# The first modulation's products turned round: weights stationary, the two conditioning vectors moving, and the stream loads dealt out between the weight loads

## The chip, the cores and the metric

One core of a Trainium2 chip runs the whole network in one launch. The metric is the device time of that launch in microseconds (us). TensorE (PE) multiplies a stationary 128x128 block, loaded into it by a weight load (PEld), by moving columns. VectorE (DVE), ScalarE (ACT) and GpSimd (POOL) do the elementwise work, and SyncE (SP) issues most transfers.

## What is computed

Four layers work on 512 latent tokens and 256 context tokens of width 1024. Ahead of each half layer both streams are normalised and modulated by shifts and scales that come from a conditioning vector: `c` for the latent tokens, `c_ctx` for the context. Cut to what matters here (layer 0, first half):

```python
sh1, sc1, ... = split(silu(c) @ ada_w + ada_b, 6)
ch1, cc1, ... = split(silu(c_ctx) @ ada_w + ada_b, 6)
xn  = rmsnorm(h, g1) * (1 + sc1) + sh1
xcn = rmsnorm(hc, g1) * (1 + cc1) + ch1
y, yc = short_conv_mixer(xn, ...), short_conv_mixer(xcn, ...)   # begins with x @ w_in
```

Nothing can be multiplied by `w_in` until the streams, their norms and the shift and scale of a channel block are there.

## The kernel before

Activations are kept channel-major, eight tiles of 128 channels per stream: `hL0` to `hL7` (128x512, the latent stream) and `hC` (128x256 each, the context). Most products are made from two rounded halves of each operand (`xh`, `xl`, `wh`, `wl`), three matmuls per product (`mm3`).

The opening of the program, up to about 60 us, is what the change touches. `run` calls `setup` and then steps a generator, `ada_first`. For each of the eight channel blocks j it loads the 256 weight columns of that block (128 for the shift, 128 for the scale) as two tiles `adaf{j}_0` and `adaf{j}_1` of 512 KB, from a pool of five buffers (tag `raw`). Before, `cwide` holds silu of the two vectors, each copied 64 times, so that it fills a 128x128 stationary block, and the 256 weight columns move past it in full float32: eight matmuls per j (the profile shows each float32 matmul as two records, each with a weight load of its own). The result has the two vectors along the partitions, so ScalarE copies it to `adarow` and TensorE turns it by two transposes. VectorE then adds the bias (`md`) and makes the gain (`gs`).

```python
raw = self.first.tile([P, KC // 2, 2 * P], F32, name=f"adaf{j}_{i}", tag="raw", bufs=5)
...
nc.tensor.matmul(acc[:, :2 * P], self.cwide[:, i * KC // 2 + k], raw[:, k], ...)
```

After `lead` blocks (2 before) `load_h` issues the loads of both streams: 8 pieces of context, 8 of x. Then three norms are begun, of the context and of the latent tokens' two halves (`norm_steps` with `first` set): ScalarE squares each channel tile (`nsq`), VectorE adds the squares (`nacc`), TensorE sums over channels with a column of ones (`nps<-ones,nacc`, 2 moving columns), POOL takes the power (`rstd`), TensorE spreads it over partitions (`nps<-identr,rstd`), and VectorE multiplies (`nt`). For each j, as soon as `md` and `gs` are there, ScalarE makes `xh`, POOL scales `nt`, and VectorE makes `xl`, three times (context, two halves).

The products of the first mixer for the context and the first latent half are issued ahead (`phase_start`, tiles `pre0` and `pre1`); they are the first consumers of `xh` and `xl`.

A scheduler orders the instructions of each engine; transfers on SP keep the program's order where the code asks for it. Each engine runs its own list in order.

Of the kernel before, what the change touches and what calls it, by code (L numbers as in the profile page):

```python
# [9 lines left out]
F32 = mybir.dt.float32  # L10
# [4 lines left out]
PSUM = bass.MemoryType.PSUM  # L15

P = 128
PRM = dict(res1=6, pg0=140, pg1=180, dir=2, wx=0, pin=0, plo=((), ()), nb=2, nl=4, lead=2, nadd='DDD', mid=(0, 0, 0), rope='PP', c1w=7, l1w=8, o1=16, s1=0, r1=6, pf0=17, pf1=33, vd1=7, ord=0, w2=12, o2=24, s2=7, v2=6, r2=8, res=2, kp=0, vp=18, t0=5, t1=4, t2=3, t3=3, ks='A', ksl='D', st='A', stl='P', qT2='A', oraw='A', qs='A', qsl='D', qT1='A', mh='A', ml='P', m='A', kT='A', vh='A', vl='P', comb='P')
KEEP = (2, 3, 4)
EARLY = (4, 5)  # L20
PADS = (32, 56)
XPAD = 48
D = 1024
KC = D // P
# [23 lines left out]
class Trunk:  # L48
# [101 lines left out]
    def cpy(self, k, out, x):  # L150
        e = PRM[k]
        if e == "A":
# [4 lines left out]
    def tt(self, k, out, a, b, op):  # L157
        (self.nc.vector if PRM[k] == "D" else self.nc.gpsimd).tensor_tensor(out, a, b, op)

# [73 lines left out]
        hC = [self.hC2[k // 2][:, k % 2, :] for k in range(KC)]  # L233
        self.h = {0: hL, 1: hC}

    def load_h(self):
        for k in range(KC):
            self.tc.keep_in_program_order(self.nc.sync.dma_start(self.h[1][k], self.A["ctx"][k]))
        for k in range(KC):
            self.tc.keep_in_program_order(self.nc.sync.dma_start(self.h[0][k], self.A["x"][k]))  # L240


    def ada_vecs(self, l, m):
# [2 lines left out]
    def ada_first(self):  # L246

        nc = self.nc
        for j in range(KC):
            if j in EARLY:  # L250
                self._fetch(True)
                self._split()
            acc = self.pb(f"adaf{j}")
            for i in range(2):
                raw = self.first.tile([P, KC // 2, 2 * P], F32, name=f"adaf{j}_{i}", tag="raw", bufs=5)
                self.tc.keep_in_program_order(nc.sync.dma_start(raw, self.A["l0_ada_first"][j, i]))
                for k in range(KC // 2):
                    nc.tensor.matmul(acc[:, :2 * P], self.cwide[:, i * KC // 2 + k], raw[:, k],
                                     start=i + k == 0, stop=i * k == KC // 2 - 1)
            row = self.ntmp("adarow")[:, :2 * P]  # L260
            nc.scalar.copy(row, acc[:, :2 * P])
            for m in range(2):
                nc.tensor.transpose(acc[:, (2 + m) * P:(3 + m) * P], row[:, m * P:(m + 1) * P], self.ident)
            cols = acc[:, 2 * P:].rearrange("p (m v e) -> p m v e", m=2, v=2)[:, :, :, 0]
            md = self.first.tile([P, 2, 2], F32, name=f"md{j}", tag="md", bufs=KC)
            nc.vector.tensor_tensor(md, cols, self.ada_b[0][:, 0:2, j:j + 1].to_broadcast([P, 2, 2]), ALU.add)
            gs = self.first.tile([P, 2], F32, name=f"gs{j}", tag="gs", bufs=KC)
            nc.vector.scalar_tensor_tensor(gs, md[:, 1, :], 1.0, self.g1[0][:, j:j + 1].to_broadcast([P, 2]),
                                           ALU.add, ALU.mult)
            self.mods1.append((md[:, 0, :], gs))  # L270
            yield
# [45 lines left out]
    def norm_steps(self, l, s, second, first):  # L317
# [16 lines left out]
        acc = self.ntmp("nacc")[:, :T]  # L334
        direct = 0 if first else PRM["dir"]
        sums = [acc]
        for k in range(KC):
# [6 lines left out]
            else:  # L344
                sq = self.ntmp("nsq")[:, :T]
                nc.scalar.activation(sq, h[k], AF.Square)
                (nc.vector if first and PRM["nadd"][2 * off // SEQ if sid == 0 else 2] == "D" else nc.gpsimd).tensor_tensor(acc, acc, sq, ALU.add)
            yield
# [27 lines left out]
        for k, (hi, lo) in enumerate(xs):  # L376
# [5 lines left out]
            else:  # L382
# [3 lines left out]
                nc.scalar.activation(hi, t1, AF.Identity, bias=sh)  # L386
            if not first and k in PRM["plo"][sid]:
                nc.scalar.activation(t1, t1, AF.Identity, bias=sh)
# [26 lines left out]
    def phase_start(self, srcs, xn, regions):  # L415

        n = PRM["nb"] if len(regions) == 2 else PRM["nl"]
        self.pre = [self.project(src, xn, parts_of(regions)[:-1], f"pre{i}", split=i >= 2) for i, src in enumerate(srcs[:n])]
# [716 lines left out]
    def run(self):  # L1135
        tc, nc = self.tc, self.nc
        es = ExitStack()
        self.setup(es)
        dp = es.enter_context(tc.tile_pool(name="arow", bufs=1, space=bass.MemoryType.DRAM))
        self.arow = dp.tile([12 * DEPTH, D], F32, name="adarows")  # L1140
        self.plan_weights()
        adac = tc.tile_pool(name="ada", bufs=1, side=self.yside)
        self.adap = adac.__enter__()
        cw = self.adap.tile([P, KC, 2, P // 2], F32, name="cwide", tag="ar", bufs=2)
        nc.vector.tensor_copy(cw, self.cpair[:, :, :, None].to_broadcast([P, KC, 2, P // 2]))
        self.cwide = cw.rearrange("p k v e -> p k (v e)")
        stc = tc.tile_pool(name="first", bufs=1, side=self.yside)
        self.first = stc.__enter__()
        self.mods1 = []
        ada = self.ada_first()  # L1150
        for _ in range(PRM['lead']):
            next(ada)
        self.load_h()
        self.xc = None
        self.xside = "left"
        self.xn_next = None
        self.next = (0, REGIONS, False)
        norms = [self.begin(s, True) for s in parts_of(REGIONS)]
        for i, nrm in enumerate(norms):
            for _ in range(PRM['mid'][i]):  # L1160
                next(ada)
            while next(nrm) != "stats":
                pass
        for j in range(KC):
            if len(self.mods1) <= j:
                next(ada)
            for nrm in norms:
                next(nrm)
        for _ in ada:
            pass  # L1170
        stc.__exit__(None, None, None)
        self.ada = self.ada_run([(0, m) for m in (2, 4, 3)])

        phases = [(0, REGIONS, False), (0, REGIONS, True), (1, REGIONS, False), (1, REGIONS, True),
                  (2, REGIONS, False), (2, (LAT,), True), (3, (LAT,), False), (3, (LAT,), True)]
        for i, (l, streams, second) in enumerate(phases):
            xn, self.xn_next = self.xn_next, None
            self.next = phases[i + 1] if i + 1 < len(phases) else None
            if l % 3 == 0 and not second:
                yc = tc.tile_pool(name=f"y{i}", bufs=1, side=self.yside)  # L1180
                y = yc.__enter__()
                self.pads(y, streams)
                self.conv_mixer(l, xn, streams, y, ticks=PRM['t0'])
            elif not second:
                (self.window_gqa if l == 1 else self.diff_attn)(xn)
            else:
                if l % 3:
                    yc = tc.tile_pool(name=f"y{i}", bufs=1, side=self.yside)
                    y = yc.__enter__()
                    self.pads(y, streams)  # L1190
                if l == 0:
                    self.ada = self.ada_run([(0, 5)] + [(1, m) for m in (1, 0, 2, 4, 3, 5)])
                if l in (1, 2):
                    adac = tc.tile_pool(name=f"ada{l}", bufs=1, side=self.yside)
                    self.adap = adac.__enter__()
                    self.ada = self.ada_run([(l + 1, m) for m in (1, 0, 2, 4, 3, 5)])
                self.ffn(l, xn, streams, y, ticks=PRM[f't{l + 1}'] if l < 3 else 3)
                self.tick(1000)
                if l == 0:
                    self.ada = self.ada_run([(0, 5)] + [(1, m) for m in (1, 0, 2, 4, 3, 5)])  # L1200
                if l in (1, 2):
                    adac.__exit__(None, None, None)
                yc.__exit__(None, None, None)
                if l == 0:
                    adac.__exit__(None, None, None)
            if self.done(f"{'ffn' if second else 'mix'}{l}"):
                if l % 3 == 0 and not second:
                    yc.__exit__(None, None, None)
                    if l == 0:
                        adac.__exit__(None, None, None)  # L1210
                break
        self.close_x()
        for k in range(KC):
            nc.sync.dma_start(self.out[k], self.h[0][k])
        if self.stop:
            for k in range(KC):
                nc.sync.dma_start(self.A["dbg"][k], self.h[1][k])
        es.close()
# [102 lines left out]
```

## Time and profile before

| | us |
|---|---|
| median of 3 runs (3159.29 to 3162.34) | 3161.04 |
| the profiled execution's own time | 3158.94 |
| its span in the trace | 3157.2 |
| PE busy (98%) | 3083.3 |
| DVE busy (69%) | 2175.6 |
| ACT busy (36%) | 1126.7 |
| POOL busy (22%) | 695.9 |

PE is busy nearly all the time, and 90% of the chain that ended last is PE. Of that chain the first 60 us are the exception: there transfers, VectorE and TensorE take turns. The mean granted clock of TensorE over the span is 0.984 of full speed.

### The profile page before, as it was taken

The numbers are of one execution on the slowest core, as the hardware profiler recorded it, in microseconds if no ns is written. First come the engines' busy times: TensorE is split into PE (matmuls) and PEld (weight loads), VectorE is DVE, ScalarE is ACT, GpSimd is POOL, SyncE is SP. The second block draws the span as 40 slices with busy tenths as digits, with TensorE's granted clock in tenths as the row PEclk, the third lists the DMA queues.
The fourth block names the chain that finished last, engine by engine and source line by source line (L and its number), as shares of the span: only waits on it lengthen the run. The fifth ranks groups of instructions, "written<-read, shape, count | busy, mean of one in ns | idle before, by whom it ended". The sixth has DMA issues, their size and how long they took to land.

```text
span 3157.2 us, 44102 instructions
## 1 busy us (share of the span) xinstructions
PE 3083.3 (98%) x17560; PEld 2706.2 (86%) x17560; DVE 2175.6 (69%) x3138; ACT 1126.7 (36%) x1864; POOL 695.9 (22%) x581
## 2 busy tenths in 40 slices
PE   8999999999999999999999999999999999999999
PEld 7889888888987888888888987788888888898888
DVE  5775888887575775876665576377788866565555
ACT  4212422222253775422222244376423333242222
POOL 2222122242024444012000134276111010010000
PEclk9999999999998999999999999999999999999999
DMA  6431434333110000323333212411355523222322
GB/s 231 147 121 54 140 118 150 127 122 100 60 63 27 28 27 1 134 94 127 105 130 114 66 58 81 153 44 44 114 194 174 192 87 107 94 87 96 103 88 81
DMA packets 105198, 322.66 MB, mean 102 GB/s; under 512 B 12576, under 2 KB 27552, under 8 KB 104992
## 3 DMA queue, kind: packets, MB, share of 16 engines
q1 hardware_dynamic: 100512, 313.26, 28.9%
q0 software_dynamic: 4480, 6.58, 1.1%
q8 instruction: 138, 2.26, 0.3%
q14 instruction: 68, 0.56, 0.1%
HBM read 311.26 MB, written 8.53 MB: 101 GB/s over the span
## 4 chain that ended last, share of the span: by engine, by line
PE 90%; DVE 5%; ACT 2%; issue 1%; DMA 1%; POOL 1%; SPq 0%; ACTq 0%; DVEq 0%; POOLq 0%
PE pd L162 9%; PE pd L163 9%; PE pd L164 9%; PE pg L162 6%; PE pg L163 6%; PE pg L164 6%; PE pa L163 6%; PE pa L162 6%; PE pa L164 6%; PE pj L683 3%; PE pj L684 3%; PE pj L685 3%; PE pre L163 1%; PE pre L164 1%; PE pre L162 1%; PE pb L162 1%
## 5 line engine op out<-in xcount | busy, mean ns | idle before, releaser
L110 ACT CAST wh<-wr 128x1024 fp32r<-128x1024 f32 x380 | 393.2, 1050 | 1192.9 <-PE pd L163 341.8
L111 DVE TENSOR_TENSOR wl<-wr,wh 128x1024 fp32r<-128x1024 f32 x380 | 490.5, 1305 | 170.9 <-ACT wh L110 167.6
L162 PE MATMUL pd<-mh,wh 128*128 128x256 f32 (+1 forms) x1712 | 563.4, 330 | 10.5 <-DVE hC L439 10.3
L163 PE MATMUL pd<-ml,wh 128*128 128x256 f32 (+1 forms) x1712 | 561.1, 328 | 0.6 <-DVE ml L1085 0.4
L164 PE MATMUL pd<-mh,wl 128*128 128x256 f32 (+1 forms) x1712 | 559.8, 327 | 0.0
L439 DVE SCALAR_TENSOR_TENSOR hL<-pd,mod,hL 128x512 f32<-128x512 f32 (+1 forms) x512 | 334.2, 660 | 249.2 <-PE pd L164 247.2
L298 POOL PARTITION_ALL_REDUCE acc<-acc x34 | 222.2, 6568 | 1098.5 <-DVE acc L296 1098.5
L162 PEld LDWEIGHTS pd<-mh,wh 128*128 128x128 f32 x1712 | 326.9, 191 | 40.8 <-DVE hC L439 10.8
L162 PE MATMUL pg<-xh,wh 128*128 128x256 f32 (+1 forms) x992 | 351.6, 354 | 1.5 <-ACT gp L585 1.5
L163 PEld LDWEIGHTS pd<-ml,wh 128*128 128x128 f32 x1712 | 327.4, 191 | 29.3 <-DVE ml L1085 2.1
L163 PE MATMUL pg<-xl,wh 128*128 128x256 f32 (+1 forms) x992 | 351.5, 354 | 0.0
L164 PE MATMUL pg<-xh,wl 128*128 128x256 f32 (+1 forms) x992 | 351.1, 354 | 0.0
L164 PEld LDWEIGHTS pd<-mh,wl 128*128 128x128 f32 x1712 | 326.7, 191 | 28.2
L163 PE MATMUL pa<-xl,wh 128*128 128x256 f32 (+1 forms) x992 | 350.8, 354 | 0.0
L162 PE MATMUL pa<-xh,wh 128*128 128x256 f32 (+1 forms) x992 | 350.6, 353 | 0.0
L164 PE MATMUL pa<-xh,wl 128*128 128x256 f32 (+1 forms) x992 | 350.2, 353 | 0.0
L296 DVE SCALAR_TENSOR_TENSOR acc<-adaw,csilu,acc 128x1024 f32<-128x1024 f32 x238 | 301.1, 1295 | 55.2 <-DMA adaw<-l_ada_w 53.5
L162 PEld LDWEIGHTS pg<-xh,wh 128*128 128x128 f32 x992 | 188.4, 190 | 27.2 <-ACT gp L585 1.7
L164 PEld LDWEIGHTS pg<-xh,wl 128*128 128x128 f32 x992 | 188.2, 190 | 25.8
L162 PEld LDWEIGHTS pa<-xh,wh 128*128 128x128 f32 x992 | 187.6, 189 | 26.3
L163 PEld LDWEIGHTS pg<-xl,wh 128*128 128x128 f32 x992 | 188.2, 190 | 25.3
L164 PEld LDWEIGHTS pa<-xh,wl 128*128 128x128 f32 x992 | 187.5, 189 | 26.1
(239 smaller groups left out, 5744.4 us busy)
## 6 DMA issues: line engine op xcount, KB each, us to landing
adaw<-l_ada_w SPq DMA_DIRECT2D x176, 512.0 KB, 4.1
wr<-l_ffn_up SPq DMA_DIRECT2D x176, 512.0 KB, 4.2
wr<-l_ffn_down SPq DMA_DIRECT2D x88, 512.0 KB, 3.5
wr<-l_sc_in SPq DMA_DIRECT2D x48, 512.0 KB, 3.6
wr<-l_da_qkv SPq DMA_DIRECT2D x24, 512.0 KB, 3.7
adaf<-l_ada_first SPq DMA_DIRECT2D x16, 512.0 KB, 5.4
wr<-l_sc_out SPq DMA_DIRECT2D x16, 512.0 KB, 3.5
wr<-l_wa_qkv SPq DMA_DIRECT2D x12, 512.0 KB, 3.5
```

The source lines that it names most:

```text
L110: keep(self.nc.scalar.copy(hi, raw))
L111: keep(self.nc.vector.tensor_tensor(lo, raw, hi.bitcast(F32), ALU.subtract))
L162: mm(ps, wh, xh, start=first, stop=False)
L163: mm(ps, wh, xl, start=False, stop=False)
L164: mm(ps, wl, xh, start=False, stop=last)
L296: keep(nc.vector.scalar_tensor_tensor(acc[v], raw, c, acc[v], ALU.mult, ALU.add))
L298: nc.gpsimd.partition_all_reduce(acc[v], acc[v], P, bass.bass_isa.ReduceOp.add)
L439: nc.vector.scalar_tensor_tensor(hk, ps, gate[sid][:, oc:oc + 1], hk, ALU.mult, ALU.add)
L683: mm(o, xh, wh[:, w], start=k == 0, stop=False)
L684: mm(o, xl, wh[:, w], start=False, stop=False)
L685: mm(o, xh, wl[:, w], start=False, stop=k == KC - 1)
```

## The change

The weights become the stationary side: each 128x128 block of `raw` is loaded, and the two vectors (`cpair`, 128x2, called `csilu` in the trace) move past it. There are now 16 matmuls per j instead of 8, and the result has channels along the partitions, as `md` wants it; the copy `adarow`, the two transposes and the tile `cwide` with its copy are gone. `lead` goes from 2 to 4, and `load_h(j)` deals the streams' pieces out by the table `LOADS`: all of the context behind the weights of block 0, and the eight pieces of x in groups of 2, 3 and 3 behind those of blocks 1, 2 and 3. Line numbers of the changed kernel stand one higher up to line 240 or so (L355 becomes L356, L162 becomes L163).

```diff
-PRM = dict(... lead=2, ...)
+PRM = dict(... lead=4, ...)
+LOADS = {0: [(1, "ctx", range(8))], 1: [(0, "x", range(2))], 2: [(0, "x", range(2, 5))], 3: [(0, "x", range(5, 8))]}
...
-    def load_h(self):
-        for k in range(KC):
-            self.tc.keep_in_program_order(self.nc.sync.dma_start(self.h[1][k], self.A["ctx"][k]))
-        for k in range(KC):
-            self.tc.keep_in_program_order(self.nc.sync.dma_start(self.h[0][k], self.A["x"][k]))
+    def load_h(self, j):
+
+        for sid, name, ks in LOADS.get(j, ()):
+            for k in ks:
+                self.tc.keep_in_program_order(self.nc.sync.dma_start(self.h[sid][k], self.A[name][k]))
...
             acc = self.pb(f"adaf{j}")
+            raws = []
             for i in range(2):
                 raw = self.first.tile([P, KC // 2, 2 * P], F32, name=f"adaf{j}_{i}", tag="raw", bufs=5)
                 self.tc.keep_in_program_order(nc.sync.dma_start(raw, self.A["l0_ada_first"][j, i]))
-                for k in range(KC // 2):
-                    nc.tensor.matmul(acc[:, :2 * P], self.cwide[:, i * KC // 2 + k], raw[:, k],
-                                     start=i + k == 0, stop=i * k == KC // 2 - 1)
-            row = self.ntmp("adarow")[:, :2 * P]
-            nc.scalar.copy(row, acc[:, :2 * P])
+                raws.append(raw)
+            self.load_h(j)
             for m in range(2):
-                nc.tensor.transpose(acc[:, (2 + m) * P:(3 + m) * P], row[:, m * P:(m + 1) * P], self.ident)
-            cols = acc[:, 2 * P:].rearrange("p (m v e) -> p m v e", m=2, v=2)[:, :, :, 0]
+                for k in range(KC):
+                    nc.tensor.matmul(acc[:, 2 * m:2 * m + 2], raws[k // (KC // 2)][:, k % (KC // 2), m * P:(m + 1) * P],
+                                     self.cpair[:, k, :], start=k == 0, stop=k == KC - 1)
+            cols = acc[:, :4].rearrange("p (m v) -> p m v", m=2)
...
-        cw = self.adap.tile([P, KC, 2, P // 2], F32, name="cwide", tag="ar", bufs=2)
-        nc.vector.tensor_copy(cw, self.cpair[:, :, :, None].to_broadcast([P, KC, 2, P // 2]))
-        self.cwide = cw.rearrange("p k v e -> p k (v e)")
...
-        self.load_h()
```

On PE, the last modulation products and the first mixer products stood before like this (`adaf_505` and `adaf_535` are the results of blocks 6 and 7, `pre_578` is `pre0`, x4 counts matmuls):

```order
L258 MATMUL adaf_505<-adaf_1_512,cwide 128x256
L258 MATMUL adaf_535<-adaf_0_536,cwide 128x256 x3
L263 MATMUL adaf_475<-identr,adarow 128x128 x2
L258 MATMUL adaf_535<-adaf_0_536,cwide 128x256
L258 MATMUL adaf_535<-adaf_1_542,cwide 128x256 x4
L162 MATMUL pre_578<-xh_0_209,wh_435 128x256
L163 MATMUL pre_578<-xl_0_210,wh_435 128x256
L164 MATMUL pre_578<-xh_0_209,wl_436 128x256
L263 MATMUL adaf_505<-identr,adarow 128x128 x2
```

and stand so now (`adaf_527` and `adaf_561` are blocks 6 and 7, `pre_608` is `pre0`):

```order
L263 MATMUL adaf_527<-csilu,adaf_1_530 128x2 x4
L263 MATMUL adaf_561<-csilu,adaf_0_562 128x2 x4
L263 MATMUL adaf_561<-csilu,adaf_1_564 128x2 x4
L263 MATMUL adaf_561<-csilu,adaf_0_562 128x2 x4
L263 MATMUL adaf_561<-csilu,adaf_1_564 128x2 x4
L163 MATMUL pre_608<-xh_0_265,wh_449 128x256
L164 MATMUL pre_608<-xl_0_266,wh_449 128x256
L165 MATMUL pre_608<-xh_0_265,wl_450 128x256
```

In both lists the first product of `pre0` stands behind the last product of block 7; the transposes that came between are gone, and each tile of weights is now read twice, for the shift and for the scale.

On SP the loads from block 1 on stood before like this (`adaf_0_137` and `adaf_1_143` are block 1, `hC` context, `hL` x):

```order
L256 DMA adaf_0_137<-l_ada_first 128x1024
L256 DMA adaf_1_143<-l_ada_first 128x1024
L238 DMA hC_100<-ctx 128x256 x2
L238 DMA hC_101<-ctx 128x256 x2
L238 DMA hC_102<-ctx 128x256 x2
L238 DMA hC_103<-ctx 128x256 x2
L240 DMA hL_91<-x 128x512
L240 DMA hL_92<-x 128x512
L240 DMA hL_93<-x 128x512
```

(five more pieces of x follow, and only then block 2) and stand so now (`adaf_0_147`, `adaf_0_174` and `adaf_0_202` are blocks 1, 2 and 3):

```order
L258 DMA adaf_0_147<-l_ada_first 128x1024
L258 DMA adaf_1_149<-l_ada_first 128x1024
L241 DMA hL_91<-x 128x512
L241 DMA hL_92<-x 128x512
L258 DMA adaf_0_174<-l_ada_first 128x1024
L95 DMA wr_447<-l_sc_in 128x1024
L258 DMA adaf_1_176<-l_ada_first 128x1024
L241 DMA hL_93<-x 128x512
L241 DMA hL_94<-x 128x512
L241 DMA hL_95<-x 128x512
L258 DMA adaf_0_202<-l_ada_first 128x1024
```

The context now comes ahead of block 1, the last three pieces of x come behind block 3, and the set of loads up to block 7 is the same.

## Rows read from the trace of the kernel before

**Rows 1.** Busy time by engine in a stretch of 20 us, granted clock, DMA share, GB/s

```profile
60.00:80.00 20.00, 20.00 (x141) 18.79 (x141) 10.15 (x13) 6.78 (x7) 0.00 (x0) 1.00 0.48 173
```

**Rows 2.** The chain that ended last, in order of time: start, us, what

```profile
20.59 3.78 PE adaf L258 x8
24.36 0.85 PE nps L178 x4
...
43.81 2.65 DVE nt L373 x8
...
55.16 0.39 PE pre L163
```

**Rows 3.** Timeline of PE: start, us, instruction, records

```profile
5.32 8.88 PE L258 MATMUL adaf<-adaf,cwide 128*128 128x256 f32 x32 [5.32 <-DMA adaf<-l_ada_first]
...
25.01 2.34 PE L258 MATMUL adaf<-adaf,cwide 128*128 128x256 f32 x8
...
46.89 0.47 PE L162 MATMUL pre<-xh,wh 128*128 128x256 f32 x1
```

**Rows 4.** Instructions of tile pre alone: PE, PEld, DVE, ACT, then clock, DMA

```profile
46.80:55.15 8.35, 6.53 (x44) 5.64 (x44) 0.00 (x0) 0.00 (x0) 1.00 0.00 0
55.15:67.26 12.11, 12.10 (x100) 12.05 (x100) 0.00 (x0) 0.79 (x1) 1.00 0.38 131
```

**Rows 5.** Groups by line and form, 0 to 60 us: busy us, mean ns

```profile
L258 PE MATMUL adaf<-adaf,cwide 128*128 128x256 f32 x128 | 33.3, 418 | 5.9 <-DMA adaf<-l_ada_first 5.9
...
L263 PE MATMUL adaf<-identr,adarow 128*128 128x128 f32 x16 | 3.1, 278 | 0.2 <-ACT adarow L261 0.2
...
L178 PE MATMUL nps<-identr,rstd 128*128 128x128 f32 x12 | 2.4, 330 | 0.0
...
L355 PE MATMUL nps<-ones,nacc 128*128 128x2 f32 x12 | 2.0, 259 | 3.9 <-DVE nacc L347 3.9
```

**Rows 6.** Timeline of PEld, two short stretches near 19.3 us

```profile
19.11 0.55 PEld L355 LDWEIGHTS nps<-ones,nacc 128*128 128x128 f32 x2
...
19.33 0.55 PEld L355 LDWEIGHTS nps<-ones,nacc 128*128 128x128 f32 x2
```

**Rows 7.** Busy time by engine (PE, PEld, DVE, ACT, POOL) in 2 us stretches, granted clock

```profile
17.00:19.00 2.00, 0.00 (x0) 0.00 (x1) 1.69 (x5) 1.55 (x5) 0.00 (x0) 1.00 1.04 404
...
21.00:23.00 2.00, 2.00 (x6) 1.55 (x6) 1.69 (x5) 1.62 (x5) 0.08 (x1) 0.50 1.01 414
...
25.00:27.00 2.00, 2.00 (x10) 1.69 (x9) 1.86 (x7) 1.74 (x5) 0.58 (x2) 0.77 1.00 389
```

**Rows 8.** The same 2-column form at 2124 us: timeline of PEld, clock there

```profile
2123.83 0.97 PEld L1069 LDWEIGHTS oss<-ones,osq 128*128 128x128 f32 x8 [1.33 <-ACT osq L1065]
...
2123.80:2124.80 1.00, 0.97 (x8) 0.97 (x8) 0.00 (x0) 1.00 0.78 217
```

**Rows 9.** Busy time by engine (PE, PEld, DVE, ACT, POOL), granted clock, layer 1's attention

```profile
1005.00:1010.00 5.00, 4.27 (x22) 3.87 (x21) 2.41 (x6) 2.11 (x6) 0.30 (x2) 0.50 0.00 0
1010.00:1015.00 5.00, 4.86 (x20) 4.36 (x21) 2.44 (x5) 2.58 (x8) 0.42 (x1) 0.50 0.00 0
```

**Rows 10.** Timeline of PE there: rounded 256-column products back to back

```profile
1007.33 0.41 PE L812 MATMUL psS<-kT2C,qT 128*128 128x256 f32 x1
1007.54 0.41 PE L814 MATMUL psS<-kT2L,qT 128*128 128x256 f32 x1
```

**Rows 11.** The chain in order of time, from one block's gain to its xl

```profile
39.37 0.61 ACT xh L380
40.07 0.49 POOL nt L381
40.58 0.72 DVE xl L391
```

**Rows 12.** DMA: a stretch by engine with GB/s; an issue, KB, us to landing

```profile
0.00:12.20 12.20, 6.88 (x24) 5.81 (x25) 1.07 (x3) 1.87 (x3) 0.77 (x8) 1.00 0.85 293
...
adaf<-l_ada_first SPq DMA_DIRECT2D x16, 512.0 KB, 5.4
```

More of the change, by code (lines that the diff above doesn't have):

```diff
@@ L17 @@
 P = 128
-PRM = dict(res1=6, pg0=140, pg1=180, dir=2, wx=0, pin=0, plo=((), ()), nb=2, nl=4, lead=2, nadd='DDD', mid=(0, 0, 0), rope='PP', c1w=7, l1w=8, o1=16, s1=0, r1=6, pf0=17, pf1=33, vd1=7, ord=0, w2=12, o2=24, s2=7, v2=6, r2=8, res=2, kp=0, vp=18, t0=5, t1=4, t2=3, t3=3, ks='A', ksl='D', st='A', stl='P', qT2='A', oraw='A', qs='A', qsl='D', qT1='A', mh='A', ml='P', m='A', kT='A', vh='A', vl='P', comb='P')
+PRM = dict(res1=6, pg0=140, pg1=180, dir=2, wx=0, pin=0, plo=((), ()), nb=2, nl=4, lead=4, nadd='DDD', mid=(0, 0, 0), rope='PP', c1w=7, l1w=8, o1=16, s1=0, r1=6, pf0=17, pf1=33, vd1=7, ord=0, w2=12, o2=24, s2=7, v2=6, r2=8, res=2, kp=0, vp=18, t0=5, t1=4, t2=3, t3=3, ks='A', ksl='D', st='A', stl='P', qT2='A', oraw='A', qs='A', qsl='D', qT1='A', mh='A', ml='P', m='A', kT='A', vh='A', vl='P', comb='P')
 KEEP = (2, 3, 4)
 EARLY = (4, 5)
+LOADS = {0: [(1, "ctx", range(8))], 1: [(0, "x", range(2))], 2: [(0, "x", range(2, 5))], 3: [(0, "x", range(5, 8))]}
 PADS = (32, 56)
```

## Prediction

> **What bounds the kernel now.** I read the busy time by stretch first. From 60 us on TensorE is busy without a gap [rows 1], so whatever the opening takes is added to the end, microsecond for microsecond, and nothing later gives it back. Only the opening has to be costed. The chain that ended last, read in order of time, shows what makes it up: weights arriving, modulation products on TensorE, then VectorE at `nt`, and from 55.16 us TensorE with the first mixer's products `pre` [rows 2]. The timeline of TensorE gives the two marks that I need: the first modulation product at 5.32 us, and the first `pre` product at 46.89 us [rows 3].
>
> `pre` does not run densely at once, since it waits for `xl`. The view of that tile alone shows 44 records up to 55.15 us, and 100 records in the 12.10 us behind [rows 4], which is 0.121 us each. Forty-four records are 5.3 us of dense work, so the opening of before is worth a `pre` that starts at 55.2 - 5.3 = **49.9 us** and never waits. That is the number to compare with.
>
> **The change, part by part.** *Removed on TensorE*: 128 records of 256 moving columns, 33.3 us busy, and 16 transpose records, 3.1 us [rows 5]. At full clock a block of 16 records took 2.34 us for half of it, so some 4.3 to 4.7 us a block [rows 3]. The removed copies `adarow` and `cwide` were off the end of the path: the first product waited for its weights, not for `cwide` [rows 3].
>
> *Added on TensorE*: 8 blocks x 16 matmuls x 2 records (a float32 matmul is two records, as in the 64 matmuls and 128 records of before [rows 5]) = 256 records, each with a weight load and only 2 moving columns. The trace has this form: the reduction `nps<-ones,nacc`. What it costs depends on the clock. At 2124 us, granted clock 1.00 (2.4 GHz), eight of them took 0.97 us, 0.12 us each [rows 8]. Near 19.3 us two pairs of loads begin 0.22 us apart [rows 6], just after TensorE had stood idle and while the granted clock was 0.50 (1.2 GHz) [rows 7]. With the rounding I take 0.215 us at the low level. So the same 256 records are 31 us at one level and 55 us at the other. The whole case hangs on the level.
>
> Which is it? The kernel starts at the bottom: nothing has run before 5.3 us. Before, the products of 256 columns brought the clock up: TensorE stood idle to 19 us, the clock was then 0.50, wide products ran back to back from 20.59 us [rows 2], and between 25 and 27 us the level rose (0.77 is a mean over the two levels, so at about 25.9 us) [rows 7]. In layer 1's attention TensorE was busy 4.27 and 4.86 us out of 5, its weight loads 3.87 and 4.36 us, and the clock stayed at 0.50 through both stretches [rows 9]. So a busy engine, and busy weight loads, are not enough there. A stage with almost nothing but weight loads moves even fewer columns than that one. No stretch of this trace has such a stage on its own, so this is a conclusion from the nearest rows: the clock stays low from 5.3 us until `pre` comes. The bounds of the term are 31 us (full clock throughout) and 56 us (0.22 each).
>
> The Trainium skill, "TensorE: Matmul & The Clock Gate", section "LDWEIGHTS (loading the stationary operand)", gives a weight load of 128 columns as 107 ns, without a word on the clock level. By it the 256 loads are an estimated 27 us at either level. The trace agrees at the high level (0.12 us) and not at the low one (0.22 us).
>
> *What lies on TensorE beside it*: the reductions (12 records) and spreads (12 records) of the three norms [rows 5] now also run at the low level: 12 x 0.215 = 2.6 us, and 12 x 0.21 (0.85 us for four at the low level [rows 2]) = 2.6 us.
>
> *Loads.* Up to block 1's second tile SP has issued 0.35 MB of constants, 2 x 1.05 MB of weights and 1.05 MB of context, 3.5 MB. At the 293 GB/s of the first 12.2 us [rows 12] it lands at 12.0 us; block 0 ends at 5.3 + 32 x 0.215 = 12.2 us. Nothing to add, 1 us at most. Later each block takes TensorE 6.9 us, and a tile needs 5.4 us to land [rows 12]. Five buffers let a tile be issued one and a half blocks (10.3 us) before it is used, so the loads hide behind TensorE. That cover holds only at the low clock: at the high one a block is 3.8 us, and one and a half blocks is 5.8 us, just about what a tile needs. The last pieces of x queue on SP behind a tile of block 3, which waits for a buffer of block 1 until about 18 us. They land some 5 us later, and their sums are asked for by TensorE only behind block 3, after 30 us: hidden.
>
> *The end of the opening.* All `pre` products stand behind block 7 on TensorE. Last product of block 7: 5.3 + 55.0 + 2.6 + 2.6 = **65.5 us**. Behind it block 7's own chain (VectorE's sums, then `xh` 0.61, `nt` 0.49, `xl` 0.72 us [rows 11]), some 2.3 us, is covered by the 21 `pre` products of channels 0 to 6 that stand ahead (4.4 us at the low level). VectorE's and ScalarE's other norm work has had 20 us more than before and is done. `pre` then moves 256 columns back to back and brings the clock up, as the wide products did in 25.9 - 20.6 = 5.3 us [rows 2, 7]. Meanwhile a product takes 0.21 us [rows 10] and not 0.121: 0.42 of the 5.3 us is lost, 2.3 us (bounds 0 and 3).
>
> *Sum.* A `pre` that never waits would start at 65.5 + 2.3 = 67.8 us, against 49.9: **+17.9 us**. On the profiled execution's own time, 3158.94, that is 3176.8. The median of the runs shown is 2.1 us higher, so I forecast **3179 us**, 0.57% slower. With the bounds (0.21 or 0.22 us a record, 0 to 1 us for the second block's weights, 0 to 3 us for the rise) this case spans 3174 to 3184.
>
> **The rivals.** (A) *The clock rises during the narrow stage*, which decides the sign. Block 7 is then limited by its transfers: 12.9 MB up to its last tile (constants, sixteen weight tiles, both streams, two mixer weights), at 293 GB/s [rows 12] by 44 us, at the 414 of 21 to 23 us [rows 7] by 31 us. From 28 us or so blocks 4 to 7 are 4 x 3.8 us on TensorE, with some 2 to 3 us of norm work between and a start that waits for the last sums of x: `pre` at 45 to 47 us. VectorE, with two sets of `nt` (2.65 us each [rows 2]) and most `xl` still to do after the last x, comes to the same. Against 49.9 that is -4 us: 3157, with 3153 as the best. For it: TensorE would be busy throughout. Against it: rows 9. It takes over if the level rises before about block 2: each block run high instead of low is worth 3.1 us, so some six of the eight must be high. The Trainium skill, the same page, section "Part 1: The HAM clock gate", says that the gate follows how busy TensorE has been; taken as busy time, that rule gives this rival, and the trace does not bear it out in [rows 9].
>
> (B) *The clock is high for part of the stage*, since 128-column spreads run in blocks 2 and 4: two to four blocks at 0.12, 6 to 12 us less, 3166 to 3173. Against: four spread records are 0.85 us [rows 2], a moment.
>
> (C) *Slower still*: TensorE also waits for loads, because the tiles are held until both halves of a block are done and SP issues in order. Five waits of 1 to 2 us: 3184 to 3189. Against: the 10.3 us of lead above.
>
> **How the numbers follow.** The forecast's case 0.67, A 0.21, B 0.07, C 0.05. About 0.2% (6 us) is what a measurement of this kernel tells from no change. A's values lie on both sides of that bound, mostly inside: 0.07 faster, 0.14 same; the rest is slower, 0.79. The forecast's own range is 3174 to 3184. For eight times in ten I need it, B and part of A and C: 3157 to 3185.
>
> **What would show it.** Right: granted clock 0.50 from the start to past 60 us, about 0.215 us from one narrow record to the next, block 7's last product near 65 us, `pre` at the low level for some microseconds, and TensorE without gaps from then on, the rest as before. Wrong: a clock that rises before 20 us, or a `pre` that begins before 50 us.

## The result, and the profile after

The changed kernel takes 3177.62 us (median of 6, 3175.48 to 3180.72) against 3160.11 us before (median of 6). The ratio is 1.0056, with a 95% interval from 1.0046 to 1.0066: slower by 17.5 us. The profiled execution has a span of 3173.7 us, 16.5 more than before.

The timeline of TensorE in the changed kernel (start, us, instruction, records) shows where:

```profile
5.06 1.84 PE L263 MATMUL adaf<-csilu,adaf 128*128 128x2 f32 x8 [5.06 <-DMA adaf<-l_ada_first]
8.01 6.99 PE L263 MATMUL adaf<-csilu,adaf 128*128 128x2 f32 x32 [1.11 <-DMA adaf<-l_ada_first]
...
44.86 21.33 PE L263 MATMUL adaf<-csilu,adaf 128*128 128x2 f32 x100
...
66.05 0.56 PE L163 MATMUL pre<-xh,wh 128*128 128x256 f32 x1
66.41 0.41 PE L164 MATMUL pre<-xl,wh 128*128 128x256 f32 x1
66.63 0.41 PE L165 MATMUL pre<-xh,wl 128*128 128x256 f32 x1
...
69.60 0.27 PE L164 MATMUL pre<-xl,wh 128*128 128x256 f32 x1
69.71 0.28 PE L165 MATMUL pre<-xh,wl 128*128 128x256 f32 x1
...
84.94 0.28 PE L163 MATMUL pb<-xh,wh 128*128 128x256 f32 x1
```

A hundred narrow records in a row take 21.33 us, 0.213 us each, and the first `pre` product comes at 66.05 us instead of 46.89 [rows 3]. From there it never waits: its 144 records are through when `pb` begins at 84.94 us. Before, `pre` ended at 67.26 us [rows 4]. The difference is 17.7 us. The `pre` products themselves are 0.21 to 0.22 us apart at first, and 0.11 to 0.12 us apart from 69.60 us on: by that spacing the clock rose there, 3.5 us after the products of 256 columns began.

The groups by form (0 to 80 us) answer to [rows 5]:

```profile
L263 PEld LDWEIGHTS adaf<-csilu,adaf 128*128 128x128 f32 x256 | 55.5, 333 | 6.2 <-issue 5.0 <-DMA adaf<-l_ada_first 1.2
L263 PE MATMUL adaf<-csilu,adaf 128*128 128x2 f32 x256 | 55.3, 350 | 6.2 <-DMA adaf<-l_ada_first 6.2
```

128 wide records and 16 transposes, 36.4 us busy, have become 256 narrow ones, 55.3 us. The busy time by engine (PE, PEld, DVE, ACT, POOL, then the granted clock) answers to [rows 7]:

```profile
30.00:40.00 10.00, 10.00 (x48) 10.00 (x49) 4.35 (x11) 2.93 (x6) 2.35 (x4) 1.00 0.53 196
...
75.00:80.00 5.00, 5.00 (x44) 5.00 (x43) 0.00 (x0) 0.00 (x0) 0.00 (x0) 1.00 0.31 121
```

TensorE and its weight loads are busy without a gap from 10 us on, with 4.8 records per us in the narrow stage, while VectorE is idle for more than half of the first stretch shown. But the column of the granted clock reads 1.00 in both rows, and I had said 0.50 for the first. Either the low clock is not the cause, or the column is not to be trusted there. The same view of the kernel before gives reason for the second:

```profile
5.00:9.00 4.00, 3.68 (x9) 3.00 (x10) 0.00 (x0) 0.00 (x0) 0.00 (x0) 1.00 0.93 355
9.00:14.00 5.00, 5.00 (x25) 4.37 (x24) 0.00 (x0) 0.37 (x1) 0.00 (x0) 1.00 1.01 335
```

The column reads 1.00 in both, yet the same products of 256 columns come at 0.41 us each up to 9 us (9 in 3.68 us) and at 0.20 us each behind (25 in 5.00 us). The experiments had to settle it.

### The profile page after: what moved, and what is told of

It reads as the page before. It is cut to its first block, busy times and chain, and to the rows that moved or that the text cites. A ratio compares the mean times of both kernels' runs of the same rounds, so it can differ in the third digit from the quotient of the medians.

```text
span 3173.7 us, 44301 instructions
## 1 busy us (share of the span) xinstructions
PE 3101.6 (98%) x17672; PEld 2731.1 (86%) x17672; DVE 2175.2 (69%) x3137; ACT 1124.0 (35%) x1856; POOL 695.4 (22%) x581
## 4 chain that ended last, share of the span: by engine, by line
PE 91%; DVE 4%; ACT 2%; issue 1%; POOL 1%; DMA 1%; SPq 0%; ACTq 0%; DVEq 0%; POOLq 0%
PE pd L163 9%; PE pd L164 9%; PE pd L165 9%; PE pg L163 6%; PE pa L164 6%; PE pg L165 6%; PE pg L164 6%; PE pa L163 6%; PE pa L165 6%; PE pj L684 3%; PE pj L685 3%; PE pj L686 3%; PE adaf L263 2%; PE pre L164 1%; PE pre L165 1%; PE pre L163 1%
## 5 line engine op out<-in xcount | busy, mean ns | idle before, releaser
L163 PE MATMUL pd<-mh,wh 128*128 128x256 f32 (+1 forms) x1712 | 563.8, 330 | 11.0 <-DVE hC L440 10.3
L163 PEld LDWEIGHTS pd<-mh,wh 128*128 128x128 f32 x1712 | 327.1, 191 | 41.0 <-DVE hC L440 10.7
L163 PE MATMUL pg<-xh,wh 128*128 128x256 f32 (+1 forms) x992 | 351.5, 354 | 1.5 <-ACT gp L586 1.5
L163 PE MATMUL pa<-xh,wh 128*128 128x256 f32 (+1 forms) x992 | 350.6, 353 | 0.0
L163 PEld LDWEIGHTS pg<-xh,wh 128*128 128x128 f32 x992 | 188.3, 190 | 27.2 <-ACT gp L586 1.7
L163 PEld LDWEIGHTS pa<-xh,wh 128*128 128x128 f32 x992 | 187.7, 189 | 26.3
```

Of the source, the lines that this page charges most:

```text
L163: mm(ps, wh, xh, start=first, stop=False)
```

## The experiments

The theory: with 2 moving columns a record the clock stays at the low level (1.2 GHz, the granted 0.50) through the whole stage, each record takes 0.21 us, and the opening ends that much later. Its rivals: a weight load in a long row of loads takes 0.21 us at any clock; or the loads, dealt out in a new order, are what costs the time.

**The products turned round, the loads as before.**

```diff
-PRM = dict(... lead=4, ...)
+PRM = dict(... lead=2, ...)
...
-LOADS = {0: [(1, "ctx", range(8))], 1: [(0, "x", range(2))], 2: [(0, "x", range(2, 5))], 3: [(0, "x", range(5, 8))]}
+LOADS = {1: [(1, "ctx", range(8)), (0, "x", range(8))]}
```

> The products turned round, but the loads in the order of before (both streams behind block 1, lead 2). Theory (TensorE's narrow records at the low clock set the end of the opening): 256 records of 0.213 us are left as they are, so the first pre product again at 65 to 67 us and the time within 2 us of the changed kernel, 3176 to 3180. Rival (the loads, held back behind the narrow stage, cost the time): pre earlier by several us and a time between 3160 and 3172.

Measured: 3180.05 us, ratio to before 1.0061 (1.0048 to 1.0073). Its timeline of TensorE:

```profile
38.75 27.73 PE L263 MATMUL adaf<-csilu,adaf 128*128 128x2 f32 x130
66.34 0.56 PE L163 MATMUL pre<-xh,wh 128*128 128x256 f32 x1
...
72.46 0.29 PE L163 MATMUL pre<-xh,wh 128*128 128x256 f32 x1
...
86.38 0.28 PE L163 MATMUL pb<-xh,wh 128*128 128x256 f32 x1
```

The records are 0.213 us again, `pre` begins at 66.34 us, and the order of the loads makes no difference to that. The slowdown is the turned product's. The time lies just above the expected 3176 to 3180 us and 2.4 us above the changed kernel, and the two intervals overlap in most of their length. In this execution `pre` runs at the low level for 6.1 us, to 72.46 us, and `pb` begins 1.4 us later than in the changed kernel.

**The loads dealt out, the products as before.** This one is the kernel before with the table `LOADS`, `load_h(j)` behind the weights of each block, and `lead=4`:

```diff
-PRM = dict(... lead=2, ...)
+PRM = dict(... lead=4, ...)
...
+            self.load_h(j)
             row = self.ntmp("adarow")[:, :2 * P]
...
-        self.load_h()
```

> The wide products of before, with the loads dealt out as in the changed kernel (lead 4). Theory: the clock comes up as before within 10 us, and the time stays within 0.2% of before, 3154 to 3166; the cost of the change is not in the loads. Rival: the loads cost the time, 3170 or more.

Measured: 3164.35 us, ratio 1.0014 (1.0005 to 1.0023). It is inside what the theory said, and not nothing: some 4 us. The timeline of TensorE shows the norms' reductions coming late, at 30.78 us for the context (19.03 us in the kernel before), and then TensorE waiting at `pre`, twice:

```profile
30.78 0.55 PE L357 MATMUL nps<-ones,nacc 128*128 128x2 f32 x4
...
46.93 0.55 PE L163 MATMUL pre<-xh,wh 128*128 128x256 f32 x1 [1.86 <-DVE md L268]
...
53.82 0.55 PE L163 MATMUL pre<-xh,wh 128*128 128x256 f32 x1 [2.80 <-DVE nt L375]
...
70.69 0.28 PE L163 MATMUL pb<-xh,wh 128*128 128x256 f32 x1
```

The busy time by engine with the granted clock, and the timeline of ScalarE, say more:

```profile
47.00:50.00 3.00, 3.00 (x14) 3.00 (x15) 2.87 (x10) 1.10 (x4) 2.26 (x4) 0.50 0.00 0
...
53.00:57.00 4.00, 3.18 (x15) 3.21 (x16) 4.00 (x10) 4.00 (x9) 3.97 (x8) 0.59 0.00 0
```

```profile
25.97 0.37 ACT L263 COPY adarow<-adaf 128x256 f32<-128x256 f32 x1 [2.25 <-PE adaf L259]
26.23 0.42 ACT L341 ACTIVATE nacc<-hC 128x256 f32<-128x256 f32 x1
```

ScalarE's first square of the context (`nacc<-hC`) stands in its list behind block 3's copy to `adarow`, and starts at 26.23 us right behind it. In the kernel before it stands behind block 1's copy and starts at 14.51 us. With `lead=4` four such copies come first, so the norms come later, and `pre`, which begins when it did (46.89 us), has to wait for VectorE. Behind each of the two waits the clock is at the low level (0.50, and 0.59 as the mean over 53 to 57 us), and 15 products are 0.21 us apart. Thirty products at 0.213 instead of 0.121 us are 2.8 us, an estimate from these rows and [rows 4], and `pb` begins 3.4 us later than in the kernel before. In the changed kernel there is no `adarow`, so this cost is not in it.

**128 columns moving.** Only the moving side of the changed kernel is altered, and what reads the result: each vector is copied 64 times, by `cwide` as in the kernel before, and moved past the same weight blocks.

```diff
-                    nc.tensor.matmul(acc[:, 2 * m:2 * m + 2], raws[k // (KC // 2)][:, k % (KC // 2), m * P:(m + 1) * P],
-                                     self.cpair[:, k, :], start=k == 0, stop=k == KC - 1)
+                    nc.tensor.matmul(acc[:, m * P:(m + 1) * P], raws[k // (KC // 2)][:, k % (KC // 2), m * P:(m + 1) * P],
+                                     self.cwide[:, k], start=k == 0, stop=k == KC - 1)
...
+        cw = self.adap.tile([P, KC, 2, P // 2], F32, name="cwide", tag="ar", bufs=2)
+        nc.vector.tensor_copy(cw, self.cpair[:, :, :, None].to_broadcast([P, KC, 2, P // 2]))
...
```

> The changed kernel, with weights stationary, but each vector copied 64 times again, so that 128 columns move past each weight block instead of 2; same 256 records, same weight loads, no transposes. In the trace of before a 128-column float32 record took 0.21 us at the low level, no more than a 2-column one, so the records cost nothing more. Theory (the clock stays low because almost nothing moves): the clock rises within some 10 us of the first product, records follow each other at 0.11 to 0.12 us, pre begins at 44 to 48 us, time 3153 to 3160. Rival (a weight load in a long row of loads takes 0.21 us whatever the clock; the column of the granted clock reads 1.00 in that stage): records stay at 0.21 us, pre at 66 us, 3177.

Measured: 3155.87 us, ratio to before 0.9988 (0.9979 to 0.9997). Its timeline of TensorE:

```profile
8.00 6.00 PE L263 MATMUL adaf<-cwide,adaf 128*128 128x128 f32 x32 [0.57 <-DMA adaf<-l_ada_first]
...
30.14 7.31 PE L263 MATMUL adaf<-cwide,adaf 128*128 128x128 f32 x64
...
44.68 0.36 PE L163 MATMUL pre<-xh,wh 128*128 128x256 f32 x1
...
63.52 0.28 PE L163 MATMUL pb<-xh,wh 128*128 128x256 f32 x1
```

Sixty-four times as many columns move, and the same 256 records with the same weight loads take 0.114 us each (7.31 us for 64) instead of 0.213. `pre` begins at 44.68 us, 21 us earlier than in the changed kernel, and `pb` at 63.52 us, 3.7 us earlier than in the kernel before. The rival of a weight load that costs 0.21 us in itself falls.

**The clock brought up first.** Twenty products of 128 columns stand ahead of block 0, on the identity; their result is not used.

```diff
+        warm = self.pb("warm")
+        for _ in range(20):
+            tc.keep_in_program_order(nc.tensor.matmul(warm[:, :P], self.ident, self.ident, start=True, stop=True))
         ada = self.ada_first()
```

> The changed kernel with 20 products of 128 moving columns ahead of block 0, on data that nothing uses, so that the clock is up before the narrow stage begins. Theory: the first narrow records follow each other at 0.11 to 0.12 us, then the column of the granted clock shows a fall to 0.50 with TensorE busy throughout, and from there 0.21 us each until pre; time 3172 to 3180 (some us won at the high level, up to 4 us lost because block 0 starts later). Rival (weight loads take 0.21 us whatever the clock): 0.21 us from the first narrow record on, no fall in the column, time 3177 to 3182. Second rival (a clock once up stays up while TensorE is busy): 0.11 to 0.12 us throughout and 3153 to 3162.

Measured: 3178.57 us, ratio 1.0060 (1.0047 to 1.0074). First its timeline of TensorE:

```profile
1.91 6.52 PE L1150 MATMUL warm<-identr 128*128 128x128 f32 x40 [1.91 <-DVE identr L212]
8.27 4.66 PE L263 MATMUL adaf<-csilu,adaf 128*128 128x2 f32 x40
...
47.49 16.64 PE L263 MATMUL adaf<-csilu,adaf 128*128 128x2 f32 x78
63.99 0.56 PE L163 MATMUL pre<-xh,wh 128*128 128x256 f32 x1
```

and then its busy time by engine (PE, PEld, DVE, ACT, POOL) with the granted clock:

```profile
9.00:12.00 3.00, 3.00 (x29) 3.00 (x29) 2.37 (x7) 2.04 (x6) 0.00 (x0) 1.00 1.01 335
12.00:15.00 3.00, 3.00 (x19) 3.00 (x18) 0.62 (x3) 0.45 (x2) 0.00 (x0) 0.58 0.99 369
15.00:18.00 3.00, 3.00 (x16) 3.00 (x15) 0.43 (x1) 1.00 (x2) 0.00 (x0) 0.50 1.01 407
...
60.00:65.00 5.00, 5.00 (x25) 5.00 (x25) 1.00 (x4) 0.44 (x1) 0.01 (x1) 0.50 0.00 0
```

This trace shows the clock's course. It is up when the narrow stage begins at 8.27 us, and its first 40 records take 4.66 us, 0.12 us each. Between 12 and 15 us the granted clock falls to 0.50, though TensorE and its weight loads were busy in every one of those microseconds. From then on a record takes 0.213 us (16.64 us for 78), the level is 0.50 between 60 and 65 us too, and `pre` begins at 63.99 us, two microseconds earlier than without the help. Both rivals named ahead of this run fall: the first records take 0.12 us and not 0.21, and the clock, once up, did not stay up. Here the column shows what the spacing of the records shows, and records 0.213 us apart stand at 0.50. So the 1.00 of the changed kernel's opening was a blank of the column and not the clock. The two microseconds do not show in the time: the two intervals overlap, and this execution's span is 2.4 us longer than the changed kernel's.

**128 columns moving, the loads as before.** The same edit of the table and of `lead` as in the first experiment, on the run with 128 columns; beside it that run again.

> Weights stationary and 128 columns moving, as in the run before, but the loads in the order of before (both streams behind block 1, lead 2). Theory (with the clock up, the opening ends with VectorE's norm work and the last transfers, and x coming earlier lets VectorE start earlier): the wide products of before lost 4 us by the dealt loads, so some 1 to 4 us are won here, 3150 to 3156, pre's last record before 63 us. Rival (block 7's last transfer sets the end, and it moves the same bytes in either order): 3154 to 3158, no difference from the run with dealt loads.

> The run with 128 moving columns and dealt loads once more, beside the one with the loads of before on the same chip: 3153 to 3159 in either theory, 0.05% to 0.2% under before.

Measured: with the loads of before 3157.98 us, ratio 0.9996 (0.9987 to 1.0005); with the dealt loads again 3155.71 us, ratio 0.9987 (0.9978 to 0.9995). The expectation that the old order would win some microseconds, with `pre` done before 63 us, was wrong: the time is no shorter, the two intervals overlap, and `pre` was done at 64.20 us. The timeline and the busy time (with the granted clock) of the run with the old order show a possible reason:

```profile
20.78 6.21 PE L263 MATMUL adaf<-cwide,adaf 128*128 128x128 f32 x28 [3.03 <-DMA adaf<-l_ada_first]
...
46.84 0.36 PE L163 MATMUL pre<-xh,wh 128*128 128x256 f32 x1
...
64.20 0.28 PE L163 MATMUL pb<-xh,wh 128*128 128x256 f32 x1
```

```profile
17.00:20.00 3.00, 0.71 (x4) 0.52 (x4) 2.80 (x9) 2.45 (x6) 0.73 (x2) 0.98 1.04 408
20.00:23.00 3.00, 2.22 (x10) 2.22 (x11) 2.79 (x9) 1.25 (x3) 0.22 (x1) 0.50 1.02 419
```

Behind block 1 the streams' 3 MB come first, TensorE waits 3.03 us for block 2, and the clock is at 0.50 behind that gap, as it was before [rows 7]. In the two traces with dealt loads no wait for weights behind the first is longer than 1.3 us, and `pb` begins at 63.52 and 62.56 us. That this is what keeps the old order from winning is argued from single executions and not shown. The run with 128 moving columns and dealt loads is the one version whose intervals lie below the kernel before, by 0.12% in the first series and 0.13% in the second.

## Why the prediction was right

**The level of the clock** was the step on which everything hung, and it held: low from the start until 3.5 us into `pre`, shown by the spacing of the records, by the run in which only the number of moving columns differs, and by the run with products ahead. What I had named as its mark, a column at 0.50, did not show, for the reason above. The stretch in layer 1's attention [rows 9] was the right evidence to go by; the fall between 12 and 15 us with TensorE busy throughout now shows it directly.

The Trainium skill, "TensorE: Matmul & The Clock Gate", section "Part 1: The HAM clock gate", lets the clock follow how busy TensorE has been. Taken as busy time, this case's trace does not agree: TensorE was busy for 3.00 of 3.00 us, and the clock fell (0.58, then 0.50).

**The price of a record**: 0.215 us predicted, 0.213 measured, 54.6 us for the 256. **The norms' reductions and spreads** run at the same 0.21 us. **The loads**: 0 to 1 us was allowed for a wait, and it came to 1.11 us, but at block 0's second tile (8.01 us) and not at block 1's. Block 7's last product was forecast for 65.5 us; `pre`, which follows it at once, began at 66.05.

**The rise at the end** was set at 5.3 us and a loss of 2.3 us; it took 3.5 us, 16 products at 0.21 instead of 0.12 us, which is 1.5 us. So `pre` was worth a start at 67.5 us, where the prediction had 67.8. That the sum came so close is in part luck: half a microsecond too little ahead of `pre` and 0.8 us too much behind it nearly cancel, and the term itself is no constant, for with the products turned alone the rise took 6.1 us. **The sum** was +17.9 us; the opening in the trace is 17.7 us longer, and the medians are 17.5 us apart.

**Two readings of rows** were wrong, and neither enters the sum. The 2.34 us for half a block [rows 3] are not at full clock, since the level rose only in the middle of that stretch; at the high level 24 records of the kernel before take 5.35 us, some 3.6 us a block. And [rows 1] shows the 20 us from 60 us on and no more: ahead of 705.78 us TensorE waits for 5.15 us in the kernel before. Its timeline of TensorE:

```profile
35.40 5.35 PE L258 MATMUL adaf<-adaf,cwide 128*128 128x256 f32 x24
...
705.78 0.58 PE L162 MATMUL pd<-mh,wh 128*128 128x256 f32 x1 [5.15 <-DVE hC L439]
```

**Microsecond for microsecond** therefore holds only up to about there. Matching the VectorE weight splits (`wl`) of the two traces one by one, the changed kernel is 17.7 us behind at most of them from 150 to 680 us, 17.0 us behind from 730 us, 19.3 us around 1500 us, and 16.5 us at the end. The stretches in which TensorE waits and the clock falls and rises, in either kernel, shift by one or two microseconds each way. These are two single executions, and whether that part repeats is left open.

Of the rivals, A (the clock rises in the narrow stage) did not occur by itself, but the run with 128 columns has the course that it described: forecast 3157 us, measured 3155.87, `pre` at 44.68 us against 45 to 47. B and C did not occur.

## What to carry to other kernels

A busy TensorE was no sign of the high clock here: a stage of 256 float32 records with 2 moving columns, each behind a full weight load, kept it busy from 8 to 66 us at the low level, 0.213 us a record. So a stage of such products is priced from rows at the low level, with the price at the high level as the rival, and so is the start of the products behind it (16 of them at 0.21 us here). More moving columns cost nothing in these records (0.21 us at the low level and 0.11 to 0.12 us at the high one, with 2 or with 128), and with 128 of them the clock was up: the same turned product with its vectors copied out was 0.12% faster than before, where with 2 columns it was 0.56% slower. And a granted clock of 1.00 at the start of a trace is checked against the spacing of the records.

## What the runs showed that I had not expected

- The granted clock read 1.00 over the whole opening, where the records were spaced as at the low level.
- Dealing the stream loads out between the weights is a loss of 0.14% with the wide products of before, and with the turned ones no loss that the intervals show.
- Two waits at `pre`, of 1.86 and 2.80 us, were each followed by 15 products at the low level, so such a wait can cost more than its own length.
- Twenty products ahead of time bring the clock up in a few microseconds (40 records in 6.52 us), and it falls again about 4 us into the narrow stage: `pre` came 2 us earlier, and the total did not differ from the changed kernel's.
